# Norm arithmetic on VectorE and ScalarE in place of GpSimd, in a two-layer diffusion step

## The chip, the cores and the metric

The kernel runs on one core of a Trainium2 chip. The metric is the device time of one execution in microseconds (us); a lower time is better. Five engines run beside one another, each through its own instructions in the order in which they were queued: TensorE (PE in the profile, its weight loads PEld), VectorE (DVE), ScalarE (ACT), GpSimd (POOL) and SyncE (SP), which issues the transfers.

## The reference, cut to what matters

One inference step of two layers on 128 context and 256 latent tokens, model width 1024. Each layer is a feed-forward half-step, a token mixer and a second feed-forward half-step, and each of the three ends in a layer norm over the 1024 channels:

```python
x = layer_norm(ALPHA * x + 0.5 * m[2] * swiglu(h, ffn1_w_in, ffn1_w_out), ln_g[0], ln_b[0])
x = layer_norm(ALPHA * x + m[5] * mixer(h), ln_g[1], ln_b[1])
x = layer_norm(ALPHA * x + 0.5 * m[8] * swiglu(h, ffn2_w_in, ffn2_w_out), ln_g[2], ln_b[2])

def layer_norm(x, g, b):
    mu = x.mean(-1, keepdims=True)
    var = jnp.mean(jnp.square(x - mu), -1, keepdims=True)
    return (x - mu) * lax.rsqrt(var + LN_EPS) * g + b
```

Everything is float32. So there are six norms in an execution, four behind a feed-forward block and two behind a mixer.

## The kernel before, in words

Activations lie with channels on partitions and the 384 tokens along the free dimension. The residual x is eight tiles `ax[0]` to `ax[7]` of 128 x 384. A weight comes from memory in units of eight 128 x 128 blocks (`raw`, 512 KB, three buffers). ScalarE rounds a unit to the matmul's format (`hi`, two buffers), VectorE takes the rest (`lo` = `raw` - `hi`, two buffers), and TensorE makes three matmuls per block: high by high (line 401), low part of the input by high weight (402), input by low weight (403). That is `Stream.fetch` and `mm3_steps`. A `hi` buffer comes free when TensorE has finished the unit before last, so each unit's `hi` and then `lo` are made while TensorE works on the unit before.

The output product of a block is eight products, one for each channel tile c: 22 blocks each behind a feed-forward block, 8 behind a mixer. `Norm.products` issues one, and `Norm.add` takes it from PSUM: VectorE adds gate times product to `ax[c]` in two instructions (context and latent columns). The norm's statistics are gathered meanwhile:

- After c = 1, 2, 3 a running sum `sa` of the first four tiles is formed. In the middle of product 4, `pilot` lets TensorE average `sa` over partitions, ScalarE scales it into `mu` (a rough mean), and `mu` is subtracted from all eight tiles (tile 4 in `add`, the others in `pilot`, tiles 5 to 7 before their products are added).
- Tiles 0 to 3 are squared and added up in `s0`; tiles 4, 5, 6 in `ss`, with tile 7 apart. `sa` starts anew with tiles 4, 5 and 6. After c = 6, `s0` is added to `ss`.
- From c = 5 on, `z` prepares the centred tiles as inputs of the next stage (`zh` on ScalarE, `zl` on VectorE), in the groups that `ZL` names. `finish` makes the statistics by matmul (`stat`, `mean`, `rs`), with matmuls of the next stage (`hd`) between them.

The 16 additions and subtractions of these steps other than tile 4's, `ss` + `sq` and the product's own are issued to GpSimd (`G`). Behind a feed-forward block GpSimd also squares tiles 0 to 3 (`on_pool`); behind a mixer ScalarE does, as it does everywhere for tiles 4 to 7.

In layer 0 the output products of both feed-forward blocks carry more: `ada_beside` loads rows of the conditioning weights (`adaw`, six buffers) and VectorE accumulates them in two sums (`acc`, 128 x 1024, two instructions for each row), 16 rows in each of these two stages. They are ordered behind the last VectorE instruction traced before them (`then(V)`). In layer 1 there are none in these stages.

Within an engine the order is fixed when the program is built: a list scheduler takes the ready instruction that was traced first, by a model of the times, and `high_priority` moves a weight unit's load, `hi` and `lo` 1500 places ahead. On the chip each engine keeps that order and waits where an input is late.

Of the kernel before, what the change touches and what calls it, by code (L numbers as in the profile page):

```python
# [11 lines left out]
AF = mybir.ActivationFunctionType  # L12
ALU = mybir.AluOpType
# [283 lines left out]
def trunk(tc, I, O, order, taps=None, stop=None):  # L297
# [3 lines left out]
    V, S, G, T = Engine(nc.vector), Engine(nc.scalar), Engine(nc.gpsimd), nc.tensor  # L301

    def then(*engines):

        st = ExitStack()
        for e in engines or (V, S, G):
            if e.last is not None:
                st.enter_context(tc.issue_after(e.last.ins))
        return st
# [14 lines left out]
    def C(name, rows=P):  # L324
        o, n = CONST_COLS[name]
        src = conM if name in ("asel", "asel2", "osel") else conA[0] if name in ("rot", "cos", "sin", "maska", "maskb") else con
        return src[:rows, o : o + n]
# [7 lines left out]
    def atp(name="at"):  # L335
        return ps("at", 3, name)
# [170 lines left out]
    ax = [act.tile([P, NTOK], F32, name=f"ax{c}") for c in range(KD)]  # L507
# [9 lines left out]
    class Norm:  # L517
# [38 lines left out]
        def add(self, c, po):  # L556
            pool = self.pool
            y = ax[c]
            for s, (a, b) in enumerate(STREAMS):
                V.scalar_tensor_tensor(out=y[:, a:b], in0=po[:, a:b], scalar=self.gate[:, c, s : s + 1], in1=y[:, a:b], op0=ALU.mult, op1=ALU.add)  # L560
            if c == 0:

                S.activation(out=pool.tile([P, 1], F32, name="warm"), in_=y[:, 0:1], func=AF.Sqrt, scale=0.0, bias=C("leps"))
            if c == 1:
                self.sa = pool.tile([P, NTOK], F32, name="sa")
                G.tensor_tensor(out=self.sa, in0=ax[0], in1=y, op=ALU.add)
            elif c in (2, 3):
                G.tensor_tensor(out=self.sa, in0=self.sa, in1=y, op=ALU.add)
            if c < 4:
                return  # L570
            if c == 4:
                V.tensor_tensor(out=y, in0=y, in1=self.mu, op=ALU.subtract)
                self.square(c)
                self.ss = self.sq
                return
            self.square(c)
            for i in ZL[c - 4]:
                with then(*((S, V) if ZT and i < 5 else (S,))):
                    self.z(i)
            if c == 7:  # L580
                return
            if c == 5:
                G.tensor_tensor(out=self.sa, in0=ax[4], in1=y, op=ALU.add)
            else:
                G.tensor_tensor(out=self.sa, in0=self.sa, in1=y, op=ALU.add)
            V.tensor_tensor(out=self.ss, in0=self.ss, in1=self.sq, op=ALU.add)
            if c == 6:
                G.tensor_tensor(out=self.ss, in0=self.ss, in1=self.s0, op=ALU.add)

        def pilot(self):  # L590

            pm = atp("pilot")
            T.matmul(pm[:, :NTOK], C("invd").to_broadcast([P, P]), self.sa, start=True, stop=True)
            self.mu = self.pool.tile([P, NTOK], F32, name="mu")
            S.activation(out=self.mu, in_=pm[:, :NTOK], func=AF.Copy, scale=2.0)
            for i in range(5, KD):
                G.tensor_tensor(out=ax[i], in0=ax[i], in1=self.mu, op=ALU.subtract)
            for i in range(4):
                G.tensor_tensor(out=ax[i], in0=ax[i], in1=self.mu, op=ALU.subtract)
                self.square(i, self.half)  # L600
                if i == 0:
                    self.s0 = self.sq
                else:
                    G.tensor_tensor(out=self.s0, in0=self.s0, in1=self.sq, op=ALU.add)

        def products(self, chunks, xs, c):

# [3 lines left out]
                    self.pilot()  # L611
            self.add(c, po)

        def square(self, c, on_pool=False):
            keep = {0: "s0", 4: "ss"}.get(c)
            self.sq = self.pool.tile([P, NTOK], F32, tag=keep or "sq", bufs=1 if keep else 2, name="sq")
            if on_pool:
                G.tensor_tensor(out=self.sq, in0=ax[c], in1=ax[c], op=ALU.mult)
            else:
                S.activation(out=self.sq, in_=ax[c], func=AF.Square)  # L620

        def finish(self, head=iter(())):

# [249 lines left out]
    def mixer(l, nxt, next_head, head):  # L873
        spill = axd.tile([P, KD, NTOK], F32, name=f"axd{l}")
        gcd = axd.tile([P, KD, NTOK], F32, name=f"gcd{l}")
        with ExitStack() as st:
# [9 lines left out]
            with tc.tile_pool(name=f"rw{l}", bufs=1) as pool:  # L886
                stream.offset, stream.parts = 100, 2
                dense[:] = [mixer_fill(l, keep, pool, w, ob, gcd), 0.0]

                def add(cost, until=None):  # L890

                    dense[1] += cost
                    while dense[1] > 0 or until is not None and until not in w:
                        with tc.issue_after(rw_last[0].ins):
                            b = next(dense[0], None)
                        if b is None:
                            break
                        dense[1] -= b

                for cost in rwkv_gen(l, pool, keep, w, oc, add):  # L900
                    add(cost)
                add(1e9)
                stream.offset, stream.parts = 1500, 1
# [851 lines left out]
    with es:  # L1755
        with tc.tile_pool(name="init", bufs=1) as pool:
# [15 lines left out]
            for c0 in range(0, KD, 2):  # L1772

                offset = 9000 - 1000 * c0
                i, cols = c0 // 4, slice(256 * (c0 % 4), 256 * (c0 % 4) + 512)
# [63 lines left out]
```

## Time and profile before

| | |
|---|---|
| median of 3 runs | 2412.66 us (2411.74 to 2422.63) |
| profiled execution | 2413.25 us, span of its instructions 2411.4 us |
| TensorE matmul busy | 2289.0 us, 95% |
| VectorE busy | 1689.8 us, 70% |
| ScalarE busy | 1066.2 us, 44% |
| GpSimd busy | 409.2 us, 17% |
| mean granted TensorE clock | 0.985 of full speed |

Busy times are those of one profiled execution and overlap between engines. A matmul's busy time includes the time that it shares with its neighbours in the array. The granted clock is given as a share of 2.4 GHz. Nearly all VectorE, ScalarE and GpSimd instructions have line 291, the helper that issues them, and are told apart by tile names.

### The profile page before, as it was taken

Reading aid. Unit: us, or ns where it says so; the run is one execution under the profiler, and the core shown is the slowest. Engines: PE = TensorE matmul, PEld = TensorE weight load, DVE = VectorE, ACT = ScalarE, POOL = GpSimd, SP = SyncE. Lnnn points to the kernel's source line nnn. Section 1 sums busy time; section 2 is a strip of 40 time slices with the busy share of each in tenths; the row PEclk is TensorE's granted clock in tenths of the full one; section 3 lists DMA queues with packets and bytes.
Section 4 is the critical chain, followed back from the end, with each engine's and each line's share of the span. In section 5 each row is a group of like instructions: output and inputs, shape, how many; then the busy total and the mean of one; then the engine's idle time right before and its main releaser. Section 6 shows DMA issues by size and latency. Waiting matters only on the chain.

```text
span 2411.4 us, 42684 instructions
## 1 busy us (share of the span) xinstructions
PE 2289.0 (95%) x17066; PEld 2098.1 (87%) x17066; DVE 1689.8 (70%) x2949; ACT 1066.2 (44%) x1962; POOL 409.2 (17%) x426
## 2 busy tenths in 40 slices
PE   8999899998899999999899999999989999999998
PEld 6999888887777788999889999888877777899997
DVE  3896877767767567876879964767787674775534
ACT  3333245655545445433243332556555454453322
POOL 1000421001122034000430003300022220530003
PEclk9999999999899999999999999999999999999999
DMA  8775544242111262665546733533321112634332
GB/s 307 246 244 184 184 115 124 90 116 71 37 61 48 72 212 88 218 205 178 168 148 218 246 127 126 153 95 93 112 71 33 55 54 81 216 122 132 123 125 85
DMA packets 125078, 324.53 MB, mean 135 GB/s; under 512 B 31568, under 2 KB 50256, under 8 KB 124880
## 3 DMA queue, kind: packets, MB, share of 16 engines
q1 hardware_dynamic: 124880, 321.81, 41.6%
q8 instruction: 134, 2.20, 0.4%
q14 instruction: 64, 0.52, 0.1%
HBM read 312.06 MB, written 9.70 MB: 133 GB/s over the span
## 4 chain that ended last, share of the span: by engine, by line
PE 74%; DVE 12%; ACT 5%; issue 3%; POOL 3%; DMA 1%; SPq 0%; ACTq 0%; POOLq 0%; DVEq 0%
PE po L403 5%; PE po L402 5%; PE po L401 5%; PE pa L385 4%; PE pa L386 4%; PE pg L385 4%; PE pg L386 4%; PE pa L387 4%; PE pg L387 4%; DVE lo L291 3%; ACT hi L291 2%; PE pz L401 2%; PE pz L402 2%; PE pz L403 2%; POOL ax L291 1%
## 5 line engine op out<-in xcount | busy, mean ns | idle before, releaser
L291 ACT ACTIVATE hi<-raw 128x1024 fp32r<-128x1024 f32 x418 | 441.7, 1058 | 743.1 <-issue 227.1
L291 DVE TENSOR_TENSOR lo<-raw,hi 128x1024 fp32r<-128x1024 f32 (+1 forms) x472 | 551.4, 1177 | 303.3 <-ACT hi L291 301.0
L291 DVE SCALAR_TENSOR_TENSOR acc<-adaw,cs,acc 128x1024 f32<-128x1024 f32 x224 | 289.0, 1330 | 0.0
L403 PE MATMUL po<-uh,lo 128*128 128x384 f32 x704 | 238.3, 338 | 10.7 <-DVE lo L291 10.5
L401 PE MATMUL po<-uh,hi 128*128 128x384 f32 x704 | 238.7, 339 | 0.0
L402 PE MATMUL po<-ul,hi 128*128 128x384 f32 x704 | 237.5, 337 | 0.0
L385 PE MATMUL pa<-zh,hi 128*128 128x384 f32 x584 | 198.7, 340 | 0.0
L386 PE MATMUL pa<-zl,hi 128*128 128x384 f32 x584 | 197.4, 338 | 0.0
L385 PE MATMUL pg<-zh,hi 128*128 128x384 f32 x584 | 197.2, 338 | 0.0
L387 PE MATMUL pa<-zh,lo 128*128 128x384 f32 x584 | 196.3, 336 | 0.6 <-DVE lo L291 0.6
L386 PE MATMUL pg<-zl,hi 128*128 128x384 f32 x584 | 196.6, 337 | 0.0
L387 PE MATMUL pg<-zh,lo 128*128 128x384 f32 x584 | 196.2, 336 | 0.0
L291 POOL TENSOR_TENSOR sa<-ax,ax 128x384 f32<-128x384 f32 x12 | 15.8, 1312 | 788.8 <-DVE ax L291 585.2
L403 PEld LDWEIGHTS po<-uh,lo 128*128 128x128 f32 x704 | 133.2, 189 | 13.2 <-DVE lo L291 13.2
L401 PE MATMUL pz<-zh,hi 128*128 128x384 f32 x352 | 127.0, 361 | 8.3 <-ACT hi L291 2.8
L401 PEld LDWEIGHTS po<-uh,hi 128*128 128x128 f32 x704 | 133.0, 189 | 2.1 <-issue 1.5
L402 PEld LDWEIGHTS po<-ul,hi 128*128 128x128 f32 x704 | 133.0, 189 | 0.5
L403 PE MATMUL pz<-zh,lo 128*128 128x384 f32 x352 | 124.8, 355 | 2.2 <-DVE lo L291 2.2
L402 PE MATMUL pz<-zl,hi 128*128 128x384 f32 x352 | 123.8, 352 | 0.0
L385 PEld LDWEIGHTS pa<-zh,hi 128*128 128x128 f32 x584 | 109.6, 188 | 4.9 <-ACT hi L291 3.7
L387 PEld LDWEIGHTS pa<-zh,lo 128*128 128x128 f32 x584 | 110.1, 189 | 0.9 <-DVE lo L291 0.9
L387 PEld LDWEIGHTS pg<-zh,lo 128*128 128x128 f32 x584 | 110.1, 189 | 0.0
(398 smaller groups left out, 5323.5 us busy)
## 6 DMA issues: line engine op xcount, KB each, us to landing
raw<-ws SPq DMA_DIRECT2D x418, 512.0 KB, 3.5
adaw<-wada SPq DMA_DIRECT2D x144, 512.0 KB, 4.5
bm<-rpb SPq DMA_DIRECT2D x64, 64.0 KB, 7.9
axd<-ax SPq DMA_DIRECT2D x16, 192.0 KB, 4.2
gcd<-gt SPq DMA_DIRECT2D x16, 192.0 KB, 4.6
gc<-gcd SPq DMA_DIRECT2D x16, 192.0 KB, 3.4
ax<-axd SPq DMA_DIRECT2D x16, 192.0 KB, 4.7
xt<-xt SPq DMA_DIRECT2D x8, 192.0 KB, 8.4
```

The costliest lines, as they stand in the source:

```text
L291: self.last = f(*a, **k)
L385: T.matmul(out, wh, xh, start=first, stop=False)
L386: T.matmul(out, wh, xl, start=False, stop=False)
L387: return T.matmul(out, wl, xh, start=False, stop=last)
L401: T.matmul(out, wh, xh, start=(k == 0), stop=False)
L402: T.matmul(out, wh, xl, start=False, stop=False)
L403: T.matmul(out, wl, xh, start=False, stop=(k == n - 1))
```

## The change

All instructions of the norm that were on GpSimd up to the statistics go to VectorE, and the squares of tiles 0 to 3 go to ScalarE in all six norms. Nothing else is edited; the number of instructions traced is the same.

```diff
@@ add
             if c == 1:
                 self.sa = pool.tile([P, NTOK], F32, name="sa")
-                G.tensor_tensor(out=self.sa, in0=ax[0], in1=y, op=ALU.add)
+                V.tensor_tensor(out=self.sa, in0=ax[0], in1=y, op=ALU.add)
             elif c in (2, 3):
-                G.tensor_tensor(out=self.sa, in0=self.sa, in1=y, op=ALU.add)
+                V.tensor_tensor(out=self.sa, in0=self.sa, in1=y, op=ALU.add)
...
             if c == 5:
-                G.tensor_tensor(out=self.sa, in0=ax[4], in1=y, op=ALU.add)
+                V.tensor_tensor(out=self.sa, in0=ax[4], in1=y, op=ALU.add)
             else:
-                G.tensor_tensor(out=self.sa, in0=self.sa, in1=y, op=ALU.add)
+                V.tensor_tensor(out=self.sa, in0=self.sa, in1=y, op=ALU.add)
             V.tensor_tensor(out=self.ss, in0=self.ss, in1=self.sq, op=ALU.add)
             if c == 6:
-                G.tensor_tensor(out=self.ss, in0=self.ss, in1=self.s0, op=ALU.add)
+                V.tensor_tensor(out=self.ss, in0=self.ss, in1=self.s0, op=ALU.add)
@@ pilot
             for i in range(5, KD):
-                G.tensor_tensor(out=ax[i], in0=ax[i], in1=self.mu, op=ALU.subtract)
+                V.tensor_tensor(out=ax[i], in0=ax[i], in1=self.mu, op=ALU.subtract)
             for i in range(4):
-                G.tensor_tensor(out=ax[i], in0=ax[i], in1=self.mu, op=ALU.subtract)
-                self.square(i, self.half)
+                V.tensor_tensor(out=ax[i], in0=ax[i], in1=self.mu, op=ALU.subtract)
+                self.square(i)
                 if i == 0:
                     self.s0 = self.sq
                 else:
-                    G.tensor_tensor(out=self.s0, in0=self.s0, in1=self.sq, op=ALU.add)
+                    V.tensor_tensor(out=self.s0, in0=self.s0, in1=self.sq, op=ALU.add)
@@ square
-        def square(self, c, on_pool=False):
+        def square(self, c):
...
-            if on_pool:
-                G.tensor_tensor(out=self.sq, in0=ax[c], in1=ax[c], op=ALU.mult)
-            else:
-                S.activation(out=self.sq, in_=ax[c], func=AF.Square)
+            S.activation(out=self.sq, in_=ax[c], func=AF.Square)
```

## Rows read from the trace of the kernel before

**Rows 1.** Busy us (and count) of each engine, clock, between product 3 and product 7
```profile
core 0: us, PE busy (x) PEld busy (x) DVE busy (x) ACT busy (x) POOL busy (x), PEclk, DMA share, GB/s
266.30:325.70 59.40, 52.31 (x298) 48.10 (x298) 53.36 (x51) 17.61 (x25) 28.40 (x18) 0.97 0.41 133
1165.70:1226.20 60.50, 53.33 (x297) 49.03 (x297) 53.30 (x50) 17.59 (x25) 28.41 (x18) 0.94 0.43 134
1474.70:1521.30 46.60, 46.60 (x268) 46.10 (x268) 24.75 (x30) 16.34 (x24) 21.27 (x18) 1.00 0.37 125
```
**Rows 2.** Waits of TensorE, layer 0's first norm: total us, times, longest
```profile
PE po L403 <- DVE lo L291: 5.1, 3, 3.1
PE ada L475 <- DVE acc L291: 1.0, 1, 1.0
PE pilot L593 <- POOL sa L291: 0.8, 1, 0.8
```
**Rows 3.** The same for layer 0's second feed-forward, its mixer, and layer 1's end
```profile
PE po L403 <- DVE lo L291: 5.4, 4, 3.2
...
PE po L403 <- DVE lo L291: 1.6, 2, 0.9
...
PE pilot L593 <- POOL sa L291: 1.0, 1, 1.0
```
**Rows 4.** VectorE by shape, 266.9 to 296.5, GpSimd beside it: busy us, mean ns
```profile
L291 DVE SCALAR_TENSOR_TENSOR acc<-adaw,cs,acc 128x1024 f32<-128x1024 f32 x8 | 14.2, 1818 | 0.0
L291 DVE TENSOR_TENSOR lo<-raw,hi 128x1024 fp32r<-128x1024 f32 x6 | 10.9, 1826 | 0.0
L291 DVE TENSOR_SCALAR acc<-adaw,cs 128x1024 f32<-128x1024 f32 x2 | 2.9, 1498 | 0.0
L291 DVE TENSOR_TENSOR ax<-ax,mu 128x384 f32<-128x384 f32 x1 | 1.4, 1390 | 0.0
```
**Rows 5.** VectorE by shape, 240 to 266.9; then all `acc`, ns min/median/max
```profile
L291 DVE TENSOR_TENSOR lo<-raw,hi 128x1024 fp32r<-128x1024 f32 x6 | 7.3, 1216 | 5.7 <-ACT hi L291 5.7
...
L291 DVE SCALAR_TENSOR_TENSOR acc<-adaw,cs,acc x224: 1270/1278/2053, 66.8 to 2278.2; 128x1024 f32<-128x1024 f32 x112
L291 DVE TENSOR_SCALAR acc<-adaw,cs x32: 744/747/1505, 65.5 to 2160.3; 128x1024 f32<-128x1024 f32 x32
```
**Rows 6.** Timeline of ScalarE, VectorE and TensorE ahead of the longest wait
```profile
285.94 1.06 ACT L291 ACTIVATE hi<-raw 128x1024 fp32r<-128x1024 f32 x1 [1.42 <-PE po L402]
...
287.60 5.74 DVE L291 SCALAR_TENSOR_TENSOR acc<-adaw,cs,acc 128x1024 f32<-128x1024 f32 x3
293.26 3.14 DVE L291 TENSOR_TENSOR lo<-raw,hi 128x1024 fp32r<-128x1024 f32 x2
...
295.33 0.44 PE L403 MATMUL po<-uh,lo 128*128 128x384 f32 x1 [3.14 <-DVE lo L291]
```
**Rows 7.** Clock behind the longest wait (columns as in Rows 1)
```profile
295.00:300.00 5.00, 4.67 (x27) 3.06 (x28) 2.52 (x5) 0.93 (x3) 0.88 (x1) 0.66 0.62 196
```
**Rows 8.** The pilot subtractions on GpSimd: busy us, mean ns, idle before
```profile
L291 POOL TENSOR_TENSOR ax<-ax,mu 128x384 f32<-128x384 f32 x42 | 57.8, 1403 | 9.4 <-ACT mu L291 9.4
```
**Rows 9.** VectorE timeline: six subtractions of the same size in `finish`
```profile
338.61 2.84 DVE L291 TENSOR_TENSOR ax<-ax,mean 128x384 f32<-128x384 f32 x6
```
**Rows 10.** TensorE's conditioning matmuls in the stretch (columns as in Rows 1)
```profile
266.30:325.70 59.40, 2.49 (x24) 0.76 (x24) 29.44 (x20) 0.97 0.41 133
```
**Rows 11.** ScalarE and VectorE timeline in layer 0's mixer norm
```profile
905.60 0.53 ACT L291 ACTIVATE sq<-ax 128x384 f32<-128x384 f32 x1 [4.37 <-POOL ax L291]
906.03 1.04 ACT L291 ACTIVATE hi<-raw 128x1024 fp32r<-128x1024 f32 x1
...
907.11 1.49 DVE L291 TENSOR_TENSOR lo<-raw,hi 128x1024 fp32r<-128x1024 f32 x1 [2.42 <-ACT hi L291]
...
910.46 0.53 ACT L291 ACTIVATE sq<-ax 128x384 f32<-128x384 f32 x1 [1.98 <-POOL sq L291]
```
**Rows 12.** GpSimd timeline, layer 1's last norm
```profile
2348.05 2.04 POOL L291 TENSOR_TENSOR sa<-sa,ax 128x384 f32<-128x384 f32 x1 [9.48 <-DVE ax L291]
```

## The prediction, made blind

> **What bounds the kernel now.** TensorE is busy for 95% of the span, so a gain can only come from stretches in which it waits or runs at its lower clock. I looked for these in three steps. First I cut the four last products of a norm out of the views by stage and set layer 0 beside layer 1 [rows 1]. From product 3's residual addition to product 7's, layer 1's first feed-forward takes 46.6 us with TensorE busy throughout, at full clock. Layer 0's two take 59.4 and 60.5 us with the same 88 blocks. The conditioning matmuls that layer 0 has besides are at most 2.5 us [rows 10]. So 59.4 - 49.1 = 10.3 us and 60.5 - 49.1 = 11.4 us are lost there.
>
> Then the waits of TensorE by releaser: it waits 5.1 us in layer 0's first norm, in three pieces, for `lo`, besides 0.8 us for GpSimd's `sa` ahead of the pilot matmul and 1.0 us for `acc` [rows 2]; the second is alike, with 5.4 us for `lo`; the mixers have 1.6 us of it, and the last norm 1.0 us for `sa` [rows 3].
>
> Last, why `lo` is late: VectorE by shape, once beside a working GpSimd and once without. The `lo` instruction takes 1.83 us instead of 1.22, `acc` 1.82 instead of 1.27, the first `acc` of a row group 1.50 instead of 0.75 [rows 4, 5]. The two engines slow each other: GpSimd's 42 subtractions average 1.40 us and its `sa` beside a `lo` took 2.04 us [rows 8, 12]. VectorE is then behind its fixed order. In the timeline `hi` was ready at 287.0, but VectorE had three `acc` (5.74 us) queued ahead of the `lo`, which began at 293.26; TensorE stood for 3.14 us [rows 6] and came back at 0.66 of full clock in the 5 us that hold the restart, a mixture of 1.2 and 2.4 GHz, which costs 5 x 0.34 = 1.7 us more [rows 7].
>
> **The change, part by part.** Sixteen instructions of 128 x 384 move from GpSimd to VectorE in each of six norms (`sa` 5, pilot subtractions 7, `s0` 3, `ss` 1), 96 in all; 16 squares (four in each feed-forward norm) move to ScalarE.
>
> *Price on VectorE.* Six subtractions of this size took 2.84 us, 0.47 each [rows 9]. Of the sixteen, 14 lie in the stretch of rows 1 (two `sa` come before it): 14 x 0.47 = 6.6 us.
>
> *What it gives back on VectorE.* In the 29.6 us of rows 4: 8 `acc` x 0.54 = 4.3, 6 `lo` x 0.61 = 3.7, 2 first `acc` x 0.75 = 1.5, and 0.9 on tile 4's subtraction (1.39 against 0.47), together 10.4 us.
>
> The sum for VectorE in layer 0's stretch is 53.4 - 10.4 + 6.6 = 49.6 us, beside TensorE's 49.1. So VectorE loses work on balance, but it becomes as full as TensorE, and nothing is left over for an order that doesn't fit. The floor of the stretch is 49.6. I allow 2.4 us above it: the 1.0 us wait for `acc` stays, because `acc` is what a full VectorE puts off, and one `lo` wait of 1.0 us (the mean of the two shorter ones of rows 2) with the refill behind it. That gives 52.0, a gain of 7.4 and 8.5 us, 15.9 together. Bounds for the pair: 21.7 (TensorE's floor in both) and nothing.
>
> The Trainium skill, page "SBUF — State Buffer", section "Who interferes with whom", says that a VectorE instruction with two SBUF inputs and a GpSimd instruction that reads SBUF exclude each other, and that the later one waits for the whole of the other. By that rule each of the 17 slowed instructions would have lost about a GpSimd instruction of 1.0 us, 17 us instead of 10.4, VectorE would come out at 43 us, and the stretch at TensorE's floor. The rows show a partial slowing (0.54 to 0.75 us each), so the sum goes by the rows.
>
> *The mixers.* There ScalarE already squares. A square stood 4.37 us behind a GpSimd subtraction, and the `hi` queued behind it started at 906.03, its `lo` at 907.11, too late; a second square stood 1.98 us for the buffer that a GpSimd addition held [rows 11]. A subtraction of 0.47 us in place of 1.40 brings the fourth, which the first square needs, 4 x 0.9 = 3.7 us earlier. Both waits should go: 1.6 us and some refill, 2.0 us for each mixer, 4.0 in all. Bounds 0 and 3 each: VectorE has 16 more instructions there, and the stage is short.
>
> *Pilot waits.* `sa` on VectorE follows the residual addition in its own queue. In the last norm it ends some 1.5 us sooner than GpSimd's 2.04 us [rows 12]: 1.0 us gained there (0 if `lo` is put ahead of it). Layer 0's 0.8 us are within the 15.9. Layer 1's first norm gains nothing, for TensorE never waits in it [rows 1].
>
> *Squares on ScalarE.* Four of 0.53 us [rows 11] in a stretch where it is busy 17.6 of 59.4 us [rows 1]: nothing, as long as they don't hold a `hi`. Cover: a unit of 24 matmuls lasts 4.17 us (46.6/268 each), and `hi` and `lo` take 1.06 + 1.22 of it, so a `lo` may be 1.9 us late at no cost. The early `sa` additions lie in VectorE's idle time (5.7 us in 26.9 ahead of the pilot [rows 5]). The moved instructions issue no transfers; queued behind them on VectorE are the next `lo` and `acc`, on ScalarE the next `hi`.
>
> Sum: 15.9 + 4.0 + 1.0 = 20.9 us off 2413.25, 2392.4 for a profiled execution. That execution lies 0.6 us above the median of three, so 2392 us.
>
> **The rivals.**
>
> *Reached in full, 2384 us.* Both layer-0 stretches at TensorE's floor (21.7), the mixers 3 each, the end 1.2: 28.9 us. For it: `acc` can be put off, and the order is built by a model without the mutual slowing, so that VectorE would for once keep its plan. Against: 49.6 against 49.1 leaves no slack. The rule of the SBUF page would lead here too.
>
> *VectorE becomes the bound, 2402 us.* If half of what a full queue can lose is lost, layer 0's stretches come to 56 us, which gives 7.9, with 1 for each mixer and 1 at the end: 10.9. For it: in-order waits for `mu` and for the squares now stand in VectorE's own queue, where `lo` and `acc` stand behind them. Against: `lo` is chosen first whenever the scheduler sees it ready, and a moved instruction lasts 0.47 us.
> The Trainium skill, page "Perfetto Trace Analysis", section "Optimizing Scalar/DVE Operations", advises to unload a saturated VectorE to ScalarE or even GpSimd, and adds that the shared read port may undo this. Its first half speaks for this rival, its second against it; rows 4 and 5 bear out the second.
>
> *Slower, 2431 us.* Squares hold `hi`. ScalarE keeps its order; a square that waits for a subtraction which stands behind three `acc` (3.8 us) keeps the next `hi` from starting. At the mixer's wait of 4.37 us each one costs 4.37 - 1.9 = 2.5 us, 16 of them 40 us, against 20.9 gained: 19 more than before. It decides from 1.9 + 20.9/16 = 3.2 us of waiting per square. For it: rows 11 show it happening. Against: there the subtraction was on the slowed GpSimd, and the `hi` are far apart (4.17 us), so that few squares can each hit another one.
>
> **How the numbers follow.** Likeliest 0.53, in full 0.17, VectorE as bound 0.21, slower 0.09. The range of 2382 to 2413 takes in the full case with a little more, the half-lost one, and reaches to no change at all; the slower case and the far ends are left out. About 0.5% (12 us) is what a measurement of this kernel can tell from no change, so the line is at 2400.6. Faster is the likeliest and the full case with a small part of the third, 0.73; the rest of the third is within 0.5%, 0.18; slower 0.09.
>
> **What would show it.** In layer 0's stretches: `lo` at 1.22 and `acc` at 1.27 us throughout, stretches of about 52 us, TensorE's waits for `lo` down from 5 us to about 1, no lower clock behind them, and a wait for `acc` that stays or grows. In the mixers no wait of a square for a subtraction over 2 us. The pilot matmul without a wait in all norms; layer 1's first stretch still 46.6. I am wrong if TensorE's waits for `lo` come back at another place of product 4 or 5, if `hi` starts late behind squares, or if `acc` is put off so far that the conditioning matmuls wait for several us.

## The result, and the profile after

The changed kernel takes 2389.81 us in the median of four runs (2388.39 to 2393.09), the kernel before 2414.12 in four runs beside it (2411.74 to 2422.63). The ratio is 0.9895, with a 95% interval of 0.9868 to 0.9922: about 25 us faster. The prediction was 2392 us. The profiled execution has a span of 2386.7 us against 2411.4, so 24.7 us are to be found between the two traces.

First the busy times of the whole span in the page of the kernel after. VectorE has 96 instructions more than before and is busy for the same time, 1689.0 us (1689.8 before); GpSimd's busy time falls by 148 us and TensorE's by 10.

```profile
PE 2279.3 (96%) x17066; PEld 2095.7 (88%) x17066; DVE 1689.0 (71%) x3045; ACT 1074.4 (45%) x1978; POOL 261.6 (11%) x314
```

The three stretches from product 3 to product 7, columns as in [rows 1]: layer 0's first and second feed-forward, layer 1's first.

```profile
266.02:315.64 49.62, 49.62 (x300) 47.74 (x298) 48.04 (x64) 19.43 (x29) 0.00 (x0) 1.00 0.47 159
1152.92:1202.51 49.59, 49.59 (x300) 47.70 (x298) 48.04 (x64) 19.44 (x29) 0.00 (x0) 1.00 0.51 162
1452.91:1499.32 46.41, 46.41 (x268) 46.15 (x267) 27.44 (x45) 18.06 (x28) 0.00 (x0) 1.00 0.38 126
```

Layer 0's stretches fall from 59.4 and 60.5 us to 49.6. TensorE is busy in all of them, at its full clock, and VectorE needs 48.0 us instead of 53.4 although it has 13 instructions more there. Layer 1's stretch is what it was.

TensorE's waits in the kernel after, from 240 to 345 us, that is around layer 0's first norm (total us, times, longest), the answer to [rows 2]:

```profile
PE hd L706 <- ACT hi L291: 1.4, 1, 1.4
PE adam L492 <- ACT adae L291: 0.5, 1, 0.5
PE hd L708 <- DVE lo L291: 0.3, 1, 0.3
```

The 5.1 us for `lo`, the 1.0 for `acc` and the 0.8 ahead of the pilot are gone; what is left lies behind the norm's products. VectorE by shape in the kernel after, 266 to 301 us, shows why, beside [rows 4, 5]:

```profile
L291 DVE SCALAR_TENSOR_TENSOR acc<-adaw,cs,acc 128x1024 f32<-128x1024 f32 x12 | 15.0, 1279 | 0.0
L291 DVE TENSOR_TENSOR lo<-raw,hi 128x1024 fp32r<-128x1024 f32 x8 | 9.8, 1219 | 0.1
L291 DVE TENSOR_TENSOR ax<-ax,mu 128x384 f32<-128x384 f32 x8 | 4.0, 551 | 0.0
L291 DVE TENSOR_SCALAR acc<-adaw,cs 128x1024 f32<-128x1024 f32 x2 | 1.4, 748 | 0.0
```

`lo` and `acc` now have the durations that they had before only where GpSimd was idle. Within 35 us VectorE does 12 `acc`, 8 `lo` and the 8 subtractions, where the old kernel did 8, 6 and 1 in 30 us. Its timeline in the kernel after shows the burst of moved subtractions and the `acc` that it puts off:

```profile
277.26 2.89 DVE L291 TENSOR_TENSOR ax<-ax,mu 128x384 f32<-128x384 f32 x6
...
309.66 6.06 DVE L291 SCALAR_TENSOR_TENSOR acc<-adaw,cs,acc 128x1024 f32<-128x1024 f32 x5
```

Six subtractions take 2.89 us from start to end, 0.48 each, the price forecast from [rows 9].

In the mixer of layer 0 I cut the norm at product 7's addition. The kernel before, from product 3 to product 7 and from there to the norm's end (the copy `hrs`), columns as in [rows 1]:

```profile
897.84:920.51 22.67, 20.91 (x113) 19.25 (x112) 15.24 (x23) 11.29 (x21) 15.99 (x13) 1.00 0.35 112
920.51:933.24 12.73, 12.12 (x67) 11.24 (x67) 10.26 (x26) 4.54 (x12) 1.00 (x1) 0.87 0.28 93
```

The kernel after, the same two parts:

```profile
889.83:908.48 18.65, 18.65 (x107) 18.39 (x106) 17.74 (x37) 11.42 (x21) 0.00 (x0) 1.00 0.38 130
908.48:919.88 11.40, 11.40 (x75) 10.87 (x74) 9.15 (x25) 4.65 (x12) 0.00 (x0) 1.00 0.27 84
```

ScalarE's timeline in that mixer of the kernel after, the answer to [rows 11]:

```profile
898.15 0.53 ACT L291 ACTIVATE sq<-ax 128x384 f32<-128x384 f32 x1 [1.37 <-DVE ax L291]
...
901.56 0.98 ACT L291 ACTIVATE sq<-ax 128x384 f32<-128x384 f32 x2 [1.86 <-DVE ax L291]
```

The waits of squares of 4.37 and 1.98 us are now 1.37 and 1.86, and TensorE is busy throughout. Of the 5.35 us gained, 4.02 lie ahead of product 7's addition and 1.33 behind it, where the granted clock was 0.87 and is now 1.00.

The norms, each from product 3's addition to its end, and the stages between them, in us:

| | before | after | difference |
|---|---|---|---|
| layer 0, first and second feed-forward | 74.78, 74.42 | 64.95, 64.85 | -19.4 |
| mixers of layer 0 and 1 | 35.40, 35.47 | 30.05, 30.04 | -10.8 |
| layer 1, first and last feed-forward | 59.27, 54.07 | 59.04, 52.79 | -1.5 |
| from layer 0's first norm to its mixer's product 3 | 556.73 | 558.86 | +2.1 |
| the same in layer 1 | 552.24 | 555.80 | +3.6 |
| all else | | | +1.3 |

The norms gave 31.7 us, more than the forecast 20.9, and 7 us were lost in stages that the change doesn't touch.

### The profile page after: what moved, and what is told of

Its sections match the earlier page's. It is cut to its first block, busy times and chain, and to the rows that moved or that the text cites. A ratio compares the mean times of both kernels' runs of the same rounds, so it can differ in the third digit from the quotient of the medians.

```text
span 2386.7 us, 42611 instructions
## 1 busy us (share of the span) xinstructions
PE 2279.3 (96%) x17066; PEld 2095.7 (88%) x17066; DVE 1689.0 (71%) x3045; ACT 1074.4 (45%) x1978; POOL 261.6 (11%) x314
## 4 chain that ended last, share of the span: by engine, by line
PE 76%; DVE 11%; ACT 5%; issue 2%; POOL 2%; DMA 1%; SPq 1%; ACTq 0%; POOLq 0%; DVEq 0%
PE po L402 6%; PE po L401 6%; PE po L403 6%; PE pa L385 4%; PE pa L386 4%; PE pg L385 4%; PE pg L386 4%; PE pa L387 4%; PE pg L387 4%; DVE lo L291 3%; PE pz L401 2%; ACT hi L291 2%; PE pz L402 2%; PE pz L403 2%; DVE gt L291 1%
## 5 line engine op out<-in xcount | busy, mean ns | idle before, releaser
L291 DVE TENSOR_TENSOR lo<-raw,hi 128x1024 fp32r<-128x1024 f32 (+1 forms) x472 | 533.7, 1140 | 273.3 <-ACT hi L291 270.7
L291 DVE SCALAR_TENSOR_TENSOR acc<-adaw,cs,acc 128x1024 f32<-128x1024 f32 x224 | 277.4, 1278 | 0.0
L291 POOL TENSOR_TENSOR ax<-ax,hrs 128x384 f32<-128x384 f32 x10 | 9.9, 1015 | 927.1 <-DMA raw<-ws 652.3
```

The lines of the kernel that those rows point to most:

```text
L291: self.last = f(*a, **k)
```

## The experiments

The forecast came out nearly right with terms that were not. Theory A: GpSimd and VectorE slow each other while both read operands, and the change gains by ending that. Its rivals are that the gain is one of order (a chain `mu`, subtractions, squares that ended late on a slow engine), and that a busy GpSimd of any kind is the trouble. "Norm" below is the length of the table above. The kernel before had medians of 2416.34 us beside e1 to e4, 2415.72 beside e5 to e7, 2415.85 beside e8 to e10 and 2413.91 beside e11.

**e1: the kernel after, with GpSimd reading beside it.**

```diff
+            junk = self.pool.tile([P, NTOK], mybir.dt.bfloat16, name="junk")
+            for _ in range(14):
+                G.tensor_tensor(out=junk, in0=self.mu, in1=self.mu, op=ALU.subtract)
```

> The changed kernel, and behind each pilot 14 GpSimd subtractions of 128 x 384 that read mu twice and write a scratch tile that nobody reads; no result depends on them. Theory A (the two engines slow each other, VectorE falls behind its fixed order): lo and acc beside them at 1.8 us again, some 10 us lost on VectorE in each of layer 0's two feed-forward norms, which now also carries the 14 moved instructions: product 3 to 7 takes 60 us or more there instead of 49.6; the mixers' norms 3 to 5 us longer; layer 1's feed-forward norms unchanged; in all 2410 to 2420 us. Rival B (the gain is that results no longer come late from GpSimd, its chain of slow steps): nothing waits for these instructions, so 2390 us, within 3.

2427.85 us, ratio 1.0059 (1.0035 to 1.0082): all of the gain is gone, and more. In e1, VectorE by shape from 266.5 to 300 us:

```profile
L291 DVE SCALAR_TENSOR_TENSOR acc<-adaw,cs,acc 128x1024 f32<-128x1024 f32 x8 | 11.7, 1489 | 0.0
L291 DVE TENSOR_TENSOR lo<-raw,hi 128x1024 fp32r<-128x1024 f32 x6 | 8.5, 1422 | 0.0
L291 DVE TENSOR_TENSOR ax<-ax,mu 128x384 f32<-128x384 f32 x8 | 8.4, 1098 | 0.0
```

The same where GpSimd runs beside it all the time, 270.3 to 288 us:

```profile
L291 DVE TENSOR_TENSOR ax<-ax,mu 128x384 f32<-128x384 f32 x7 | 7.9, 1177 | 0.0
L291 DVE SCALAR_TENSOR_TENSOR acc<-adaw,cs,acc 128x1024 f32<-128x1024 f32 x3 | 5.5, 1846 | 0.0
L291 DVE TENSOR_TENSOR lo<-raw,hi 128x1024 fp32r<-128x1024 f32 x2 | 3.7, 1842 | 0.0
L291 DVE TENSOR_SCALAR acc<-adaw,cs 128x1024 f32<-128x1024 f32 x2 | 2.5, 1313 | 0.0
```

GpSimd's one group in layer 0's first norm of e1 (busy us, mean ns, idle before it):

```profile
L291 POOL TENSOR_TENSOR junk<-mu 128x384 bf16<-128x384 f32 x14 | 17.9, 1277 | 229.8 <-ACT mu L291 228.7
```

And TensorE's one wait in that stretch of e1:

```profile
PE po L403 <- DVE lo L291: 3.4, 2, 2.6
```

The 14 instructions of GpSimd lie beside 14 of VectorE, and each of these takes 0.57 to 0.63 us more than in the kernel after (0.55, 1.28, 1.22 and 0.75 us there), whether it is short or long. Nobody waits for GpSimd's subtractions, so the loss comes by the slowing alone. Norms: 72.2 and 71.7 us in layer 0, 36.5 in both mixers. Layer 1's, which neither kernel had trouble with, now lose too, 63.2 and 58.4. The timeline of VectorE and ScalarE in layer 1's first norm of e1 shows how:

```profile
1478.37 6.06 DVE L291 TENSOR_TENSOR ax<-ax,mu 128x384 f32<-128x384 f32 x6 [0.78 <-ACT mu L291]
1484.35 1.84 DVE L291 TENSOR_TENSOR lo<-raw,hi 128x1024 fp32r<-128x1024 f32 x1
...
1488.48 0.53 ACT L291 ACTIVATE sq<-ax 128x384 f32<-128x384 f32 x1 [3.50 <-DVE ax L291]
1488.92 1.05 ACT L291 ACTIVATE hi<-raw 128x1024 fp32r<-128x1024 f32 x1
```

The six subtractions take 6.06 us instead of 2.89 with a `lo` queued behind them, and a square that waits 3.50 us keeps the `hi` behind it from starting. That is the rival "slower" of the prediction, past its limit of 3.2 us.

**e2: the same with writes alone.** In place of the subtractions, 56 memsets of 128 x 192 in each norm (`G.memset(junk, 0.0)`).

> As the run with reading instructions, but behind each pilot 56 GpSimd memsets of 128 x 192, which write a scratch tile and read nothing. If the slowing comes from GpSimd's reads (A, by way of the shared read side): lo at 1.22 and acc at 1.27 us beside them, 2390 us, within 3. If any busy GpSimd slows VectorE (A, by way of writes or of both): lo and acc clearly longer, and 2400 us or more.

2425.12 us, ratio 1.0052 (1.0033 to 1.0070), but it doesn't answer the question. Nothing tied the memsets to the norms, and they ran elsewhere, the first at 51.1 us. The norms were those of the kernel after, and the 35 us lay in other stages. The trace shows no slowing there: the 12 `lo` that lie wholly beside memsets take 1.22 us on average. But the memsets stand between GpSimd's own instructions, and TensorE waits 6.7 us for GpSimd's `zl`, 8.6 us for the `hi` of the same product and 6.5 us for ScalarE's `mh`, where the kernel after has none of these waits.

**e5: the same, tied to the norm.** GpSimd reads `mu` once, and the memsets follow in order.

```diff
+            G.tensor_tensor(out=junk, in0=self.mu[:, : NTOK // 2], in1=self.mu[:, : NTOK // 2], op=ALU.subtract)
+            for _ in range(56):
+                with then(G):
+                    G.memset(junk, 0.0)
```

> The kernel after, and in every norm GpSimd first reads mu once and then writes zeros 56 times into a 128x192 tile of its own that nobody reads, ordered one behind the other, so that they lie beside the norm's products (the memsets of e2 ran elsewhere). Theory A (what slows VectorE is that both engines read and write operands at once, as in e1's subtractions): a memset has no operand to read, so lo stays at 1.22 us and acc at 1.28 beside them, layer 0's FFN norms stay at 64.9 us from the first statistics to the norm's end, the mixers' at 30.05, and the time within 0.4% of 2390 us. Theory B (any busy GpSimd slows VectorE): lo and acc rise towards the 1.42 and 1.49 of e1, layer 0's FFN norms to 68 us or more, the time to 2410 or more.

2391.19 us, ratio 0.9892 (0.9875 to 0.9910), as the kernel after. GpSimd's timeline in e5 behind the pilot:

```profile
271.76 0.68 POOL L291 TENSOR_TENSOR junk<-mu 128x192 f32<-128x192 f32 x1 [231.52 <-ACT mu L291]
272.50 3.75 POOL L291 MEMSET junk<- 128x192 f32 x12
```

VectorE by shape in e5, 268 to 303 us:

```profile
L291 DVE SCALAR_TENSOR_TENSOR acc<-adaw,cs,acc 128x1024 f32<-128x1024 f32 x12 | 15.2, 1296 | 0.0
L291 DVE TENSOR_TENSOR lo<-raw,hi 128x1024 fp32r<-128x1024 f32 x8 | 9.7, 1214 | 0.0
```

`lo` at 1.21 and `acc` at 1.30 us beside a GpSimd that writes: Theory A holds, and it is the reading that costs. The 8 `acc` of e5 that lie wholly beside memsets take 1.27 us; only the first `acc` of a row group is a little longer there, 0.80 us against 0.75.

**e3 and e4: the change in the feed-forward norms alone, and in the mixers' alone.** In e3 one line picks the engine (e4 has `False`); the squares follow it:

```diff
+            E = V if self.half == True else G
-                V.tensor_tensor(out=ax[i], in0=ax[i], in1=self.mu, op=ALU.subtract)
+                E.tensor_tensor(out=ax[i], in0=ax[i], in1=self.mu, op=ALU.subtract)
...
```

> The change in the four feed-forward norms alone; the mixers' norms as before. A: layer 0's two norms gain about 9.7 us each from the pilot to the scale's copy, the last norm 1.3, and the mixers' norms stay at 35.4 us: 2393 us. If the changed order in the feed-forward norms costs later stages something (the 2 to 4 us by which both mixer stages were longer in the one profile of the changed kernel), it shows here too: 2397 us.

> The change in the two mixers' norms alone; the feed-forward norms as before. A: 5.4 us less in each of the two, 30.0 instead of 35.4 us from product 3 to the scale's copy, half of it behind the statistics, where TensorE no longer runs at its lower clock: 2403 us. The forecast on record gave 2.0 each: 2410 us.

e3: 2397.22 us, ratio 0.9935 (0.9910 to 0.9959); e4: 2407.30 us, 0.9967 (0.9949 to 0.9984). As ratios of 2413 us that is 15.7 and 8.0 us, together 23.7, against 25.3 for the whole: the parts add up within their intervals. Each set of norms reached its length of the kernel after (64.9 twice, 30.05 twice) and left the other at its length of before, but for 0.7 us at most. e3 lies at its second reading, 2397: the last norm gained 0.8 of the 1.3 us, and in its one profile the two mixer stages last 1116.5 us instead of 1109.0, though the mixers are those of before. e4 lies between its two forecasts.

**e6, e7 and e8: which of the moved instructions.** All three start from the kernel before. e6 moves the pilot subtractions and the additions of `s0` to VectorE, and the mixers' squares no longer wait for GpSimd; sums and squares stay:

```diff
-                G.tensor_tensor(out=ax[i], in0=ax[i], in1=self.mu, op=ALU.subtract)
+                V.tensor_tensor(out=ax[i], in0=ax[i], in1=self.mu, op=ALU.subtract)
...
-                    G.tensor_tensor(out=self.s0, in0=self.s0, in1=self.sq, op=ALU.add)
+                    V.tensor_tensor(out=self.s0, in0=self.s0, in1=self.sq, op=ALU.add)
```

> The kernel before with the pilot subtractions and the adds of s0 on VectorE alone: the partial sums, ss + s0 and the four squares of an FFN norm stay on GpSimd, so some 10 of its 18 instructions in a norm stay and 14 of VectorE's additions are all there but 5. Theory A (the gain goes with the number of GpSimd instructions that lie beside VectorE's): about half of the 9.8 us comes in each of layer 0's FFN norms (about 70 us from the first statistics to the end, against 74.8 and 64.9), the mixers gain most of their 5.4 us since their squares no longer wait for GpSimd, in all 2400 us. Theory B (it is the chain mu, subtractions, squares on GpSimd, that the end waits for): the whole gain without the sums, 66 us or less a norm, about 2392.

2391.16 us, ratio 0.9898 (0.9876 to 0.9920): not to be told from the whole change. Norms 66.0 twice in layer 0 and 30.1 twice in the mixers, so the share that I expected for the sums and squares isn't there; Theory B's numbers hold, though e1 slows down without its chain. Layer 0's first stretch in e6, columns as in [rows 1]:

```profile
268.59:320.67 52.08, 50.02 (x298) 47.27 (x297) 50.76 (x61) 17.60 (x25) 9.09 (x8) 1.00 0.45 154
```

VectorE by shape in e6, 268.6 to 303 us:

```profile
L291 DVE SCALAR_TENSOR_TENSOR acc<-adaw,cs,acc 128x1024 f32<-128x1024 f32 x10 | 12.4, 1274 | 0.0
L291 DVE TENSOR_TENSOR lo<-raw,hi 128x1024 fp32r<-128x1024 f32 x7 | 9.9, 1414 | 0.1
```

TensorE's two longest waits in e6's stretch:

```profile
PE ada L475 <- DVE acc L291: 1.0, 1, 1.0
PE pilot L593 <- POOL sa L291: 0.8, 1, 0.8
```

Still 9.1 us of GpSimd and a `lo` of 1.41 us, and of the 5.1 us of waiting for `lo` 0.3 are left: beside 28 us of GpSimd VectorE stays behind its order, beside 9 it does not. The two waits left are those of [rows 2], and they are most of the 2.5 us that e6 lacks in the stretch.

e7 moves the four squares of a feed-forward norm to ScalarE, and nothing else:

```diff
-            if on_pool:
-                G.tensor_tensor(out=self.sq, in0=ax[c], in1=ax[c], op=ALU.mult)
-            else:
-                S.activation(out=self.sq, in_=ax[c], func=AF.Square)
+            S.activation(out=self.sq, in_=ax[c], func=AF.Square)
```

> The kernel before with only the four squares of each FFN norm moved from GpSimd to ScalarE; pilot subtractions and sums stay on GpSimd, so the mixers are those of before. Theory A (slowing by GpSimd beside VectorE, 4 of its 18 instructions in a norm gone): layer 0's FFN norms 72 to 73.5 us (74.8 before), in all 2408 to 2412. Theory B (ScalarE's squares then wait for GpSimd's subtractions and hold the copies to hi behind them, the rival of the prediction that comes out slower): waits of squares on GpSimd of over 2 us on ScalarE, hi and lo late, TensorE's waits for lo grow, a norm of 75 to 77 us, 2415 or more.

2411.30 us, ratio 0.9985 (0.9969 to 1.0001), between the two. Layer 0's norms fall to 71.3 and 70.7 us, a little more than A had; layer 1's rise from 59.3 to 61.5 and from 54.1 to 56.5, which is B. The longest wait of a square on ScalarE in layer 0's first stretch of e7:

```profile
ACT sq L291 <- POOL ax L291: 6.5, 1, 6.5
```

TensorE's longest wait in the same stretch of e7:

```profile
PE po L401 <- ACT hi L291: 2.3, 1, 2.3
```

And layer 1's first stretch in e7, columns as in [rows 1]:

```profile
1460.74:1509.59 48.85, 47.26 (x268) 45.96 (x267) 23.72 (x30) 18.09 (x28) 14.95 (x14) 1.00 0.35 118
```

The square that stands 6.5 us behind a GpSimd subtraction holds `hi`, and TensorE waits 2.3 us. As long as the subtractions stay on GpSimd, squares on ScalarE are not free.

e8, the complement of e6, moves the five partial sums and `ss + s0` alone:

```diff
-                G.tensor_tensor(out=self.sa, in0=ax[0], in1=y, op=ALU.add)
+                V.tensor_tensor(out=self.sa, in0=ax[0], in1=y, op=ALU.add)
...
```

> The kernel before with only the five partial sums and ss + s0 of each norm on VectorE; pilot subtractions, adds of s0 and the FFN norms' squares stay on GpSimd. The complement of e6, which left the sums on GpSimd and had the whole gain. Theory A (the gain hangs on the chain mu, subtractions, squares on GpSimd and the slowing beside it): the burst of 7 subtractions, 4 squares and 3 adds stays as it is, layer 0's FFN norms gain at most the wait for the last sum before the pilot (0.8 to 1.0 us) and stay at 73 us or more, the mixers at 35.4; 2408 to 2416. Theory B (each GpSimd instruction taken away gives its share, 6 of 18): 71.5 us a norm in layer 0, about 2406.

2406.62 us, ratio 0.9969 (0.9951 to 0.9986). My A falls: norms 71.9 and 70.4 us, mixers 32.8 instead of 35.4, in all the 2406 of B. Layer 0's first stretch in e8, columns as in [rows 1]:

```profile
266.11:324.36 58.25, 52.34 (x300) 48.62 (x298) 52.99 (x55) 17.58 (x25) 24.00 (x14) 0.97 0.40 135
```

VectorE by shape in e8, 267 to 303 us:

```profile
L291 DVE SCALAR_TENSOR_TENSOR acc<-adaw,cs,acc 128x1024 f32<-128x1024 f32 x9 | 16.3, 1843 | 0.0
L291 DVE TENSOR_TENSOR lo<-raw,hi 128x1024 fp32r<-128x1024 f32 x7 | 11.3, 1625 | 0.3 <-ACT hi L291 0.3
```

The burst is as slow as before. In layer 0's first norm e6 gains 8.8 us and e8 2.9, together 11.7, with 9.8 to be had: the two overlap, and the subtractions with the additions of `s0` bring nine tenths of it.

**e9 to e11: the kernel after again, and one step further.** In the kernel after VectorE stands twice 5.1 us, at the start of the two feed-forward stages that follow layer 0's mixer and layer 0's second feed-forward, until GpSimd has read the old `ag`; the kernel before has the same two waits. e10 gives `ag` two buffers and e11 three; e9 is the kernel after.

```diff
-            self.ag = ag = lpool.tile([P, 2, KD], F32, tag="ag", name="ag")
+            self.ag = ag = lpool.tile([P, 2, KD], F32, tag="ag", bufs=3, name="ag")
```

> The kernel after once more, so that e10 has it on its own chip: 2390 us. By the reading that the mixer stages' length goes with the granted clock of the execution and not with the change, its two mixer stages (from a norm's end to the next mixer's third statistics) come out between 550 and 561 us each with the same count of matmuls, and TensorE's busy time in them moves with that length, as it did in the seven profiles so far.

> The kernel after with two buffers for ag, the scaled gain and bias of a norm's residual: VectorE stands 5.1 us twice before it writes ag anew, because GpSimd still reads the old one, and TensorE's first product behind it waits 2.0 us for lo. Theory A (the wait is on the path): the two waits go, TensorE's two waits of 2.0 us and the lower clock behind them too, 2382 to 2386, 4 to 8 us below e9. Theory B (TensorE has work enough, or the lo that is late is held by something else): as e9 within 2 us.

> The kernel after with three buffers for ag. With two, one of VectorE's two waits of 5.1 us stayed in e10: the scheduler wrote the second ag of layer 0 earlier, and the next one then waited in the same place of layer 0's second feed-forward stage for GpSimd's reads of the one before. Theory A (each wait costs TensorE its 2.0 us and the clock behind it, as the 3.4 us that e10 gained in one stage): the second goes too, with TensorE's second wait of 2.0 us for lo, another 3 us, 2380 to 2382. Theory B (the wait goes but something else is late there): as e10, 2384.

e9: 2388.90 us, ratio 0.9895 (0.9876 to 0.9914), with mixer stages of 559.5 and 555.5 us, as expected. e10: 2383.63 us, 0.9869 (0.9847 to 0.9892). e11: 2379.34 us, 0.9854 (0.9832 to 0.9876). In e10 one of the two waits stayed, and the gain is 5.3 us by medians. VectorE's group of `ag` in the kernel after, with the idle time before it at the end of the row:

```profile
L291 DVE TENSOR_SCALAR ag<-vec 128x8 f32<-128x8 f32 x10 | 1.2, 167 | 19.1 <-POOL ax L291 10.2 <-DMA vec<-vec 8.9
```

TensorE's longest waits in the product behind it, in the kernel after (besides one of 0.8 us for `zl`):

```profile
PE first L387 <- DVE lo L291: 4.0, 2, 2.0
```

The same group in e11:

```profile
L291 DVE TENSOR_SCALAR ag<-vec 128x8 f32<-128x8 f32 x10 | 1.2, 167 | 9.4 <-DMA vec<-vec 9.4
```

And what TensorE waits for in that product in e11:

```profile
PE first L386 <- DVE zl L291: 1.6, 3, 0.9
```

Both waits for GpSimd are gone, and the two feed-forward stages that held them are 3.8 and 3.3 us shorter (229.25 and 231.87 us against 233.05 and 235.18 in e9, from a norm's end to product 3's addition). By medians e11 is 9.6 us under e9, which ran beside another group of runs of the kernel before; as ratios the two lie 0.0041 apart with their intervals just touching. e11 has the lowest median here, but its interval overlaps that of e10.

## Why the prediction was right, and where it was not

*The slowing and what it costs: right.* `lo` at 1.22 and `acc` at 1.28 us throughout, no lower clock in the stretches, no wait ahead of the pilot, layer 1's first stretch 46.4 us: as forecast. e1 and e5 show the cause.

*Layer 0's stretches, 15.9 us: right in kind, too small.* They gained 9.8 and 10.9, 20.7 in all (19.4 by the norms' ends, since the second gave 1.4 back behind product 7). Two terms were mis-sized. The price of 0.47 us an instruction held (0.48), but what VectorE gets back is 53.4 - 48.0 + 14 x 0.48 = 12.0 us and not 10.4. The instructions that I had counted give 10.2 over the whole stretch. I counted those of 29.6 us alone and so left out two `sq` additions (0.91 us each before, 0.55 now) and four `zl` (0.67 and 0.48), 1.5 us together. And the 2.4 us that I allowed above the floor, for an `acc` and a `lo` that come late, were not needed: the waits are not there. I took a full queue to mean that its order would not fit; it put five `acc` off to 309.66 us, and TensorE waited for none of them. That the stretch came out at 49.6 us, the floor of the forecast, is luck: that floor was VectorE's, which needs 48.0, and it is TensorE, for which I had 49.1, that fills the stretch.

*The mixers, 2.0 us each: the step that failed most.* They gave 5.4 each, outside the bound of 3. The two waits of squares shrank as forecast. I priced only TensorE's waits for `lo` (1.6 us) and 0.4 us behind them. A stage cut in two shows the rest. In the norm of before TensorE stood for 2.4 us in all (35.40 less 33.04 us busy; 0.6 of it for `sv`, ahead of the statistics), and now for nothing. Behind product 7's addition it ran at a granted clock of 0.87, a mixture of 1.2 and 2.4 GHz, for 12.7 us, which costs 12.7 x 0.13 = 1.7 us by the same sum that I made in layer 0. The remaining 1.3 us is busy time at full clock: in front of product 7's addition 113 matmuls took 20.9 us, 0.185 each, and 107 take 18.65 now, 0.174 each. How much of this came by the slowed `lo` (1.55 us on average in that norm, 1.22 now) and how much by the squares' waits for GpSimd, no run separates.

*The last norm, 1.0 us:* 1.3. *Squares free:* yes, with the subtractions on VectorE (e7).

*The rule of mutual exclusion.* The Trainium skill, page "SBUF — State Buffer", section "Who interferes with whom", has VectorE's instructions with two SBUF inputs contend with a GpSimd instruction that reads, not with one that only writes. e5 agrees: `lo` kept 1.21 us beside memsets. The page also has the later instruction wait for the whole of the other, and the prediction called the rows a partial slowing instead. e1 speaks for taking turns: 14 instructions of VectorE beside 14 of GpSimd, each longer by about the same 0.6 us, and over the whole execution (1738.5 - 1689.0)/84 = 0.59 us of VectorE's busy time for each GpSimd subtraction added. What doesn't hold is the price of 1.0 us that the prediction worked out by the rule: of a GpSimd instruction of 1.0 us (1017 ns for `sa` in e6), VectorE loses some 0.6. So the sum by the rows was right to stay under the 17 us, though their losses are better read as a fixed time for each instruction than as a share. The norms, with 31.7 us, gave more than the 28.9 of the rival "in full".

*The sum, 20.9 us: right by two errors.* The norms gave 11 us more than forecast, and the stages between them took 7 back, which I had at nothing. That the two nearly cancel is luck. The mixer stage of layer 1 (a norm's end to product 3's addition of the mixer's norm), columns as in [rows 1], in the kernel before:

```profile
1534.01:2086.25 552.24, 515.34 (x4886) 444.49 (x4885) 391.20 (x882) 297.68 (x623) 99.22 (x125) 0.99 0.31 94
```

The same stage in the kernel after:

```profile
1511.95:2067.75 555.80, 518.21 (x4886) 446.40 (x4885) 389.66 (x884) 297.80 (x623) 99.00 (x123) 0.98 0.31 94
```

And in e7:

```profile
1522.27:2082.09 559.82, 524.55 (x4887) 452.13 (x4885) 390.74 (x882) 298.23 (x623) 98.33 (x125) 0.97 0.29 93
```

The matmuls are the same in number (the one more lies on the edge of the stretch), and VectorE and ScalarE work the same time. TensorE is busy 515.3, 518.2 and 524.6 us for them, while the granted clock falls from 0.99 to 0.97. By the clock's record the stage holds 13.7, 20.5 and 34.1 us at 1.2 GHz, which cost half their length. Without that and without TensorE's idle time (36.9, 37.6 and 35.3 us), 508.5, 508.0 and 507.5 us are left. So in layer 1 it is the clock that makes the stage longer, and no new wait. Why it is granted less stays open. Layer 0's mixer stage is another case: it has 23.9 us at 1.2 GHz in both kernels, and 1.8 of its 2.1 us are idle time of TensorE, 38.1 us instead of 36.3, in several short waits. The two mixer stages together last 1114.4 to 1115.1 us in the five kernels that have all of the after kernel's norms without a reader beside them (the kernel after, e5, e9 to e11), and 1109.0 and 1108.5 in the kernel before and e4. That looks as if the norms decided it, but e1, whose norms do wait, has 1119.4, e3 has 1116.5 with the mixers' norms of before, and e6 has 1111.6 with nearly the whole gain. No experiment tells these apart.

## What to carry to other kernels

Where two engines read the same memory at once, cost an instruction by the duration that it has beside the other, and look whether an idle helper is really free: here 96 instructions moved to the busier engine left its busy time where it was. Move the burst on which a chain hangs first (here seven subtractions and three additions, which alone came as far as the whole change); squares moved without it gained in layer 0 and lost in layer 1. And when TensorE's waits are priced, add the time it spends at a lower clock behind them, stage by stage.

## What the runs showed of the hardware

GpSimd slows VectorE when it reads: beside subtractions of 128 x 384 (e1) each of 14 VectorE instructions took about 0.6 us longer, whatever its length, `lo` 1.84 instead of 1.22 us and the subtraction 1.18 instead of 0.55; not when it only writes, `lo` 1.21 us beside memsets (e5). VectorE's residual addition, which takes one operand from TensorE's accumulators, was not slowed: 0.47 us for 128 x 256 in the six cases of e1 and the ten of the kernel before that lay wholly beside such instructions of GpSimd, and 0.48 in the kernel after. And the same 4,886 matmuls of a mixer stage kept TensorE busy for 515 to 525 us, by the clock that it was granted; two executions of the kernel after came out alike in length (555.80 and 555.47 us in layer 1, 558.86 and 559.50 in layer 0).
